# High and low part of the streamed operand in one product, for gates and scores of a two-layer mixer

## The chip, the core and the metric

The kernel runs on one core of a Trainium2 chip. The metric is the device time of one execution in microseconds, the median of several runs. One execution is also recorded by the hardware profiler; all rows shown are of that one.

## The reference, cut to what matters

Two layers over 256 tokens and 2048 channels. Each layer normalises, projects, runs an mLSTM (8 heads, keys of 128, values of 256) beside a gated linear recurrence, and projects back. The change concerns two places of the mLSTM: the input and forget gates of all heads, and the scores.

```python
p = u @ w_in
qk, v, o, z_a, ig, fg, xb, z_b = jnp.split(p, SPLIT_AT, axis=-1)
...
i_pre = ig.astype(f32) + i_bias.astype(f32)
log_f = jax.nn.log_sigmoid(fg.astype(f32) + f_bias.astype(f32))
...
sc = jnp.einsum("bhtk,bhsk->bhts", qc, kc) * jnp.exp(dmat - m_t[..., None])
num = jnp.einsum("bhts,bhsv->bhtv", sc, vc) + ...
```

`ig` and `fg` are 8 columns each of the projection. The kernel does not go chunk by chunk: it takes all 256 tokens at once, with the decay of each pair of tokens in a matrix E.

## The kernel before, in words

**Products in three parts.** Every float32 operand of TensorE is split into a high part H (rounded to the TensorE format) and a low part L, the rest. A product is H·H + H·L + L·H, summed in PSUM. ScalarE casts the high part (`wH`, line 308), VectorE subtracts for the low part (`wL`, L168, the line of the helper `tt_`).

**The stream of weights.** The weights come as units of 1 MB through SyncE's DMA queue into `raw`. A unit has two half-units, and a half-unit of a projection is 12 products of 512 columns (L332). `prepare` makes the casts and splits up to three half-units ahead of TensorE, into four buffers each for `wH` and `wL`; in the opening the first eight half-units take two casts and two splits each. A cast waits until TensorE has finished with the buffer of four half-units earlier. TensorE takes the half-units in a fixed order (`_sequence`): for each layer four groups of two heads, each with o, qk, v, xb, z, zb and the block gates (L753, 24 products of 256 a half-unit) and the output projection.

**Work beside the stream.** What follows a projection is written as generators in a queue `bg`; `pump` advances them after each half-unit, `yield` gives a cost against a budget, and `"wait"` lets the next one run. The framework then orders each engine's instructions by its own priorities, so a generator's operations stand between casts and splits in an order that the code does not fix alone.

**Gates of the heads.** `gates` lays the 16 gate columns of the weights out as 104 columns `gwp`: H of i at 0, H of f at 32, L of i at 64, L of f at 96. `gates_mm` multiplies them with the activations (`st["x"]`, 16 tiles of high and low part) into `ps_g`. `gates_gen` sums rows 0 and 64 (i) and 32 and 96 (f) after scaling by `rb`, the token's norm; then a logarithm of the sigmoid (tiles `scs`), a running sum, a running maximum, and its negative nG. nG goes out to DRAM through GpSimd's queue (`nG_d`, L538) and returns broadcast to all partitions (`nb`, L566). `e_gen` makes E from `nb` and the columns `at`: VectorE (L176), the exponential on ScalarE (L578), and the causal mask on GpSimd (L581).

**Scores.** In `qk_post`, for each of a group's two heads, six products give `ps_S`: keys are the stationary operand, queries stream, 128 keys against their 128 and 256 later tokens. VectorE multiplies by the scale and E into `Pt` (L171 is the line of the helper `stt`). `Pt` is split into PH (ScalarE, L651) and PL (VectorE), which the products `ps_n` with the values read. `ps_g`, `ps_S`, `ps_n` and the block gates' `ps_gt` take turns in four PSUM banks (`aux`).

Other names in the rows: `qc` and `xc` are the short convolutions, `vL` the low part of the values, `blk` and `tok` the transposes to channels.

Of the kernel before, what the change touches and what calls it, by code (L numbers as in the profile page):

```python
# [12 lines left out]
ALU = mybir.AluOpType  # L13
# [5 lines left out]
T = 256  # L19
KT = D // P  # L20
# [4 lines left out]
DK_SCALE = 128.0 ** -0.5  # L25
# [59 lines left out]
def tile_trunk(ctx, tc, x, xt, par, gw, gb, ws, final_g, out):  # L85
    nc = tc.nc
    V, S, G, PE = nc.vector, nc.scalar, nc.gpsimd, nc.tensor
# [9 lines left out]
    st = {"nload": 0, "credit": 0.0, "nprep": 0, "pair": 0, "aux": 0}  # L97

    def aux(name):
        st["aux"] = 1 - st["aux"]  # L100
        return psum.tile([P, 512], F32, tag=f"aux{st['aux']}", name=name, bufs=2)
# [55 lines left out]
    gbs = const.tile([NH, DEPTH, 2], F32, name="gbs")  # L157
# [9 lines left out]
    def tt_(o, a, b, op):  # L167
        return V.tensor_tensor(out=o, in0=a, in1=b, op=op)  # L168

    def stt(o, a, s, b, op0, op1):  # L170
        return V.scalar_tensor_tensor(out=o, in0=a, scalar=s, in1=b, op0=op0, op1=op1)  # L171

    def ts_(o, a, s1, op0, s2=None, op1=None):
        if s2 is None:
            return V.tensor_scalar(out=o, in0=a, scalar1=s1, scalar2=None, op0=op0)
        return V.tensor_scalar(out=o, in0=a, scalar1=s1, scalar2=s2, op0=op0, op1=op1)  # L176
# [37 lines left out]
    def order(ins, prev):  # L214
        tc.add_manual_dep(ins.ins, prev.ins.name,
                          mybir.DependencyInfo(mybir.DependencyClass.NoSync, mybir.DependencyReason.DATA),
                          reason="an order of the program")
# [276 lines left out]

    def gates_mm(l):
        ps = aux("ps_g")
        o = ps[0:104, 0:T]
        for kt in range(KT):
            gw_ = st["gwp"][kt // 8][:, kt % 8, :]
            m = PE.matmul(o, gw_, st["x"][:, kt, 0, :], start=kt == 0, stop=False)  # L500
            if kt == 0:
                order(m, st["mm"])
            PE.matmul(o, gw_, st["x"][:, kt, 1, :], start=False, stop=kt == KT - 1)  # L503
        st["ps_g"] = ps

    def gates_gen(l):
        ps, rb = st["ps_g"], st["rb", l]

        scs = work.tile([P, 8, T], F32, tag="xcs", name="scs")

        def sc(nm):
            return scs[0:NH, "ifzsd".index(nm), :]

        gi, x_ = sc("i"), sc("f")
        t_ = sc("z")
        tt_(x_, ps[32:40, 0:T], rb[32:40, :], ALU.mult)
        tt_(t_, ps[96:104, 0:T], rb[96:104, :], ALU.mult)
        stt(x_, x_, gbs[:, l, 1:2], t_, ALU.add, ALU.add)
        t_ = sc("s")
        tt_(gi, ps[0:8, 0:T], rb[0:8, :], ALU.mult)  # L520
        tt_(t_, ps[64:72, 0:T], rb[64:72, :], ALU.mult)
        tt_(gi, gi, t_, ALU.add)
        yield 0.6
        q = log1p_exp_half(x_, sc)
        yield 4
        ts_(q, q, -2.0, ALU.mult)
        stt(x_, x_, 0.0, q, ALU.min, ALU.add)
        Fc = sc("z")
        V.tensor_tensor_scan(out=Fc, data0=ones.bitcast(F32)[0:NH, 0:1].to_broadcast([NH, T]), data1=x_, initial=0.0, op0=ALU.mult, op1=ALU.add)
        sT = scs[0:64, 5, :]  # L530
        G.memset(sT, 0.0)
        stt(sT[0:8, :], gi, gbs[:, l, 0:1], Fc, ALU.add, ALU.subtract)
        Gm = sc("s")
        V.tensor_tensor_scan(out=Gm, data0=sT[0:8, :], data1=sT[0:8, :], initial=0.0, op0=ALU.max, op1=ALU.max)
        stt(sT[32:40, :], Fc, -1.0, Gm, ALU.mult, ALU.subtract)
        nG = sc("d")
        ts_(nG, Gm, -1.0, ALU.mult)
        nc.gpsimd.dma_start(out=nG_d[l], in_=nG)  # L538
        sb = scs[0:64, 6, :]
        V.transpose(out=sb, in_=sT)  # L540
        st["sb"] = sb
        st["nG", l] = True
        yield 3
# [42 lines left out]
    def mm3(o, aH, aL, bH, bL, first=True, last=True):  # L586
        PE.matmul(o, aH, bH, start=first, stop=False)  # L587
        PE.matmul(o, aH, bL, start=False, stop=False)  # L588
        PE.matmul(o, aL, bH, start=False, stop=last)  # L589
# [25 lines left out]
    def qk_post(l, g, acc):  # L615
        bg.append(e_gen(l, g))
        fr = to_channels(l, acc)

        def gen():
            for _ in range(LANDING):  # L620
                yield "wait"
            ch = joined(fr)
            yield 0.3
            qc = work.tile([P, 4, T], F32, tag="c4", name="qc", bufs=2)
            sg = work.tile([P, 4, T], F32, tag="sC", name="qsg")
            for ct in range(4):
                conv(ch, qc, ct, O_QKW + 4 * (8 * (ct % 2) + 2 * g + ct // 2), l, None)
                yield 1.2
            S.activation(out=sg, in_=qc, func=AF.Sigmoid)
            tt_(qc, qc, sg, ALU.mult)  # L630
            yield 1.2
            q = work.tile([P, 4, 2, T], F32R, tag="qs", name="qks")
            S.copy(out=q[:, :, 0, :], in_=qc)
            tt_(q[:, :, 1, :], qc, q.bitcast(F32)[:, :, 0, :], ALU.subtract)
            yield 1.2
            for _ in range(3):
                yield "wait"
            while ("E", l, g) not in st or ("v", l, g) not in st:
                yield "wait"
            E, em, so, (vH, vL) = st["E", l, g], st["em", l], st["so", l, g], st["v", l, g]  # L640
            Pt = work.tile([P, 2, 384], F32, tag="Pt", name="Pt")
            for h in range(2):
                ps = aux("ps_S")
                for o_, ss_, ts__ in ((256, slice(128, 256), slice(128, 256)), (0, slice(0, 128), slice(0, 256))):
                    mm3(ps[:, o_ : o_ + ts__.stop - ts__.start], q[:, 2 * h + 1, 0, ss_], q[:, 2 * h + 1, 1, ss_],
                        q[:, 2 * h, 0, ts__], q[:, 2 * h, 1, ts__])
                stt(Pt[:, h, :], ps[:, 0:384], DK_SCALE, E[:, h, :], ALU.mult, ALU.mult)
                yield 0.5
            PH = work.tile([P, 2, 384], F32R, tag="sD", name="PH")
            PL = work.tile([P, 2, 384], F32R, tag="sC", name="PL")  # L650
            S.copy(out=PH, in_=Pt)  # L651
            tt_(PL, Pt, PH.bitcast(F32), ALU.subtract)
            yield 1.0
            for _ in range(3):
                yield "wait"
            hh = work.tile([P, 2, 2, 256], F32, tag="sE", name="hh")
            mv = small.tile([P, 2, 2, 2], F32, tag="mv", name="mv", bufs=1)
            for h in range(2):
                pns = [aux("ps_n") for _ in range(2)]
                for t in range(2):  # L660
                    o = pns[t][:, 0:258]
                    a = slice(P * t, P * t + P)
                    mm3(o, PH[:, h, a], PL[:, h, a], vH[:, 0, h, :], vL[:, 0, h, :], last=t == 0)
                    if t == 1:
                        mm3(o, PH[:, h, 256:384], PL[:, h, 256:384], vH[:, 1, h, :], vL[:, 1, h, :], first=False)
                for t in range(2):
                    pn = pns[t]
                    dn = small.tile([P, 1], F32, tag="dn", name="dn")
                    stt(dn, pn[:, 256:257], -1.0, em[:, t, 2 * g + h : 2 * g + h + 1], ALU.mult, ALU.max)
                    tt_(dn, dn, pn[:, 256:257], ALU.max)  # L670
                    V.reciprocal(out=dn, in_=dn)
                    stt(hh[:, t, h, :], pn[:, 0:256], dn, so[:, t, 256 * h : 256 * h + 256], ALU.mult, ALU.mult)
                    bs = small.tile([P, 6], F32, tag="bs", name="bs")
                    V.bn_stats(out=bs, in_=hh[:, t, h, :])
                    V.bn_aggr(out=mv[:, t, h, :], in_=bs)
                    yield 1.1
            sd = small.tile([P, 2, 2], F32, tag="sd", name="sd", bufs=1)
            order(S.activation(out=sd, in_=mv[:, :, :, 1], func=AF.Sqrt, bias=epst), st["wH"])
            V.reciprocal(out=sd, in_=sd)
            for hd in range(2):  # L680
                for t in range(2):
                    ts_(hh[:, t, hd, :], hh[:, t, hd, :], mv[:, t, hd, 0:1], ALU.subtract, sd[:, t, hd : hd + 1],
                        ALU.mult)
            st["hn", l, g] = hh
            yield 1.0
        bg.append(gen())

    def z_post(l, g, acc):
# [396 lines left out]
    for item in dict.fromkeys(i for i, _ in seq):  # L1085
        kind, l, g = item[0], item[1], item[-1]
# [125 lines left out]
```

## Time and profile before

| | us |
|---|---|
| median of 3 runs | 1493.76 (1493.61 to 1494.64) |
| span of the profiled execution | 1491.3 |
| TensorE busy | 1481.6 |
| VectorE busy | 1050.9 |
| ScalarE busy | 925.8 |

The profiled execution's own time outside its span is not given apart; its span, from the first to the last instruction, is 2.5 us under the median of the runs. TensorE's granted clock is 0.998 of full speed over the span. Rows of the chain of work give start, duration and what ran. Rows of a timeline give start, duration, engine, line, operation, output <- input, and in brackets the idle time of the engine before it with what ended it. Rows by group give shape, count, busy time, mean duration in ns, and idle time before. A product's duration in a timeline includes its run through the array, which overlaps the next product; what a product takes on the path is seen in the chain.

### The profile page before, as it was taken

To read this page: it belongs to the slowest core of one execution; us is meant where nothing else is said; L and a number is where in the kernel's file an instruction comes from. 1 tells how busy PE (TensorE), PEld (TensorE's weight loads), DVE (VectorE), ACT (ScalarE), POOL (GpSimd) and SP (SyncE) were. 2 spreads that over 40 slices of the span, in tenths; PEclk is the share of its full clock that TensorE was granted. 3 is DMA by queue.
4 is the path that set the end of the run, shared out by engine and by line. 5 is a ranking of instruction groups with operands and counts; after the bars stand their busy time and mean duration, and the time that the engine had idled before them with its cause. 6 is when DMAs were issued, how large, how long until landed. Compare 5 with 4: busy or idle time off the path is not lost.

```text
span 1491.3 us, 18541 instructions
## 1 busy us (share of the span) xinstructions
PE 1481.6 (99%) x6894; PEld 1241.1 (83%) x6894; DVE 1050.9 (70%) x1406; ACT 925.8 (62%) x1167; POOL 81.8 (5%) x154
## 2 busy tenths in 40 slices
PE   9999999999999999999999999999999999999997
PEld 8888888888888888888888888888888888888886
DVE  6778976675567855778867798765855678556785
ACT  7656864575565855658575667645755567555675
POOL 0010100000000000000000101000000000000002
PEclk9999999999999999999999999999999999999999
DMA  9866766866677666876886666568666777577783
GB/s 337 296 224 221 227 221 208 254 224 216 199 239 232 217 225 217 258 258 226 270 277 195 231 219 240 205 205 253 223 223 216 238 223 234 200 229 265 231 282 111
DMA packets 91370, 345.66 MB, mean 232 GB/s; under 512 B 9984, under 2 KB 30480, under 8 KB 69776
## 3 DMA queue, kind: packets, MB, share of 16 engines
q1 hardware_dynamic: 79472, 306.44, 60.2%
q0 software_dynamic: 9344, 33.58, 9.1%
q10 hardware_dynamic: 2464, 4.47, 0.8%
q8 instruction: 54, 0.88, 0.2%
q14 instruction: 36, 0.29, 0.0%
HBM read 307.20 MB, written 37.24 MB: 231 GB/s over the span
## 4 chain that ended last, share of the span: by engine, by line
PE 99%; ACT 0%; DVE 0%; issue 0%; ACTq 0%
PE acc L332 89%; PE ps_gt L753 3%; PE acc L345 1%; PE acc L995 1%; PE acc L994 1%; PE acc L996 1%; PE acc_x L995 0%; PE acc_x L994 0%; PE acc_x L996 0%; PE ps_blank L110 0%; PE ps_n L589 0%; PE ps_n L587 0%; PE ps_n L588 0%; PE ps_g L500 0%; PE ps_g L503 0%; PE ps_S L588 0%
## 5 line engine op out<-in xcount | busy, mean ns | idle before, releaser
L332 PE MATMUL acc<-wH,x_s 128*128 128x512 f32 x3008 | 930.0, 389 | 0.0
L168 DVE TENSOR_TENSOR wL<-raw,wH 128x1024 fp32r<-128x1024 f32 (+1 forms) x532 | 636.5, 1204 | 341.8 <-ACT wH L308 341.3
L308 ACT CAST wH<-raw 128x1024 fp32r<-128x1024 f32 (+1 forms) x532 | 548.0, 1037 | 398.5 <-PE acc L332 367.6
L332 PEld LDWEIGHTS acc<-wH,x_s 128*128 128x128 f32 x3008 | 564.6, 188 | 116.9
L332 PE MATMUL acc<-wL,x_s 128*128 128x512 f32 x1504 | 583.9, 389 | 0.0
L332 PEld LDWEIGHTS acc<-wL,x_s 128*128 128x128 f32 x1504 | 282.3, 188 | 58.1
L332 PE MATMUL acc<-wH,yaH 128*128 128x512 f32 x224 | 87.4, 390 | 0.0
L332 PE MATMUL acc<-wH,ybL 128*128 128x512 f32 x224 | 87.3, 390 | 0.0
L332 PE MATMUL acc<-wH,yaL 128*128 128x512 f32 x224 | 87.2, 389 | 0.0
L332 PE MATMUL acc<-wL,ybH 128*128 128x512 f32 x224 | 87.2, 389 | 0.0
L332 PE MATMUL acc<-wH,ybH 128*128 128x512 f32 x224 | 87.2, 389 | 0.0
L332 PE MATMUL acc<-wL,yaH 128*128 128x512 f32 x224 | 87.2, 389 | 0.0
L332 PEld LDWEIGHTS acc<-wH,ybL 128*128 128x128 f32 x224 | 42.0, 188 | 9.1 <-DVE ybL L168 0.3
L332 PEld LDWEIGHTS acc<-wH,yaL 128*128 128x128 f32 x224 | 42.1, 188 | 9.0
L332 PEld LDWEIGHTS acc<-wH,ybH 128*128 128x128 f32 x224 | 42.1, 188 | 8.5
L332 PEld LDWEIGHTS acc<-wL,ybH 128*128 128x128 f32 x224 | 42.0, 188 | 8.5
L332 PEld LDWEIGHTS acc<-wL,yaH 128*128 128x128 f32 x224 | 42.1, 188 | 8.4
L332 PEld LDWEIGHTS acc<-wH,yaH 128*128 128x128 f32 x224 | 42.0, 188 | 8.2
L446 DVE STREAM_TRANSPOSE blk<-tok 128x1024 f32<-128x1024 f32 x33 | 40.8, 1237 | 11.0 <-ACT tok L436 11.0
L436 ACT ACTIVATE tok<-acc,rstd 128x512 f32<-128x512 f32 x46 | 29.1, 684 | 30.6 <-PE acc L332 30.6
L450 POOL DMA_DIRECT2D fr<-moved x34 | 18.9, 556 | 506.5 <-DMA moved<-blk 260.1
L892 ACT COPY stage<-acc 128x1024 f32<-128x1024 f32 x24 | 24.4, 1017 | 35.5 <-PE acc L332 35.3
(209 smaller groups left out, 1308.5 us busy)
## 6 DMA issues: line engine op xcount, KB each, us to landing
raw<-in_ws_dram SPq DMA_DIRECT2D x168, 1024.0 KB, 5.1
raw<-in_ws_dram SPq DMA_DIRECT2D x190, 512.0 KB, 4.9
fr<-moved POOLq DMA_DIRECT2D x34, 512.0 KB, 6.0
moved<-blk SPq DMA_DIRECT2D x132, 128.0 KB, 2.6
x_d<-stage POOLq DMA_DIRECT2D x24, 512.0 KB, 5.4
x_d<-x_acc ACTq DMA_DIRECT2D x8, 512.0 KB, 8.4
x_acc<-x_d SPq DMA_DIRECT2D x8, 512.0 KB, 4.4
xp<-in_xt_dram SPq DMA_DIRECT2D x8, 256.0 KB, 7.2
```

What stands on the lines that cost most here:

```text
L168: return V.tensor_tensor(out=o, in0=a, in1=b, op=op)
L308: st["wH"] = S.copy(out=H[:, o], in_=r[:, o])
L332: st["mm"] = PE.matmul(o, a_[:, kt, P * t : P * t + P], W[:, k], start=b, stop=z)
L345: PE.matmul(ps[:, ct, T * part : 2 * T], W[:, k, P * ct : P * ct + P], moving, start=first and k == 0 and part == 0, stop=last and k == 3 ...
L436: S.activation(out=by_block(tok, t), in_=acc[:, t, :].rearrange("p (c m j) -> p c m j", c=4, m=4), func=AF.Copy, scale=rstd[:, t : t + 1])
L446: V.transpose(out=blk.rearrange("p m n -> p (m n)"), in_=tok.rearrange("p m c t j -> p (m c t j)"))
L450: back.dma_start(out=fr.rearrange("p a c t i -> p a (c t i)"), in_=moved)
L753: PE.matmul(o, W[:, ib, jl], xs[:, ib, a, :], start=j == 0 and i == 0 and W is Hv and a == 0, stop=i == 1 and W is Lv, skip_group_check=True)
L892: S.copy(out=stage, in_=ps)
L994: PE.matmul(o, yH[:, kt, tsl], Hv[:, k, cs], start=start and k == 0, stop=False)
L995: PE.matmul(o, yH[:, kt, tsl], Lv[:, k, cs], start=False, stop=False)
L996: PE.matmul(o, yL[:, kt, tsl], Hv[:, k, cs], start=False, stop=stop and k == 1)
```

## The change

The high and the low part of the streamed operand lie next to each other, so one product with the same stationary operand streams both. Their results land in two halves of a PSUM bank, and the halves are added afterwards.

```diff
     def gates_mm(l):
...
-            m = PE.matmul(o, gw_, st["x"][:, kt, 0, :], start=kt == 0, stop=False)
+            m = PE.matmul(ps[0:104].rearrange("p (a t) -> p a t", a=2), gw_, st["x"][:, kt], start=kt == 0, stop=kt == KT - 1)
...
-            PE.matmul(o, gw_, st["x"][:, kt, 1, :], start=False, stop=kt == KT - 1)
...
     def gates_gen(l):
...
+        def summed(o, t_, r):
+            tt_(o, ps[r : r + 8, 0:T], rb[r : r + 8, :], ALU.mult)
+            for q0, c0 in ((r, T), (64 + r, 0)):
+                tt_(t_, ps[q0 : q0 + 8, c0 : c0 + T], rb[q0 : q0 + 8, :], ALU.mult)
+                yield t_
+
         gi, x_ = sc("i"), sc("f")
-        t_ = sc("z")
-        tt_(x_, ps[32:40, 0:T], rb[32:40, :], ALU.mult)
-        tt_(t_, ps[96:104, 0:T], rb[96:104, :], ALU.mult)
-        stt(x_, x_, gbs[:, l, 1:2], t_, ALU.add, ALU.add)
-        t_ = sc("s")
-        tt_(gi, ps[0:8, 0:T], rb[0:8, :], ALU.mult)
-        tt_(t_, ps[64:72, 0:T], rb[64:72, :], ALU.mult)
-        tt_(gi, gi, t_, ALU.add)
+        for t_ in summed(x_, sc("z"), 32):
+            tt_(x_, x_, t_, ALU.add)
+        ts_(x_, x_, gbs[:, l, 1:2], ALU.add)
+        for t_ in summed(gi, sc("s"), 0):
+            tt_(gi, gi, t_, ALU.add)
...
             for h in range(2):
-                ps = aux("ps_S")
-                for o_, ss_, ts__ in ((256, slice(128, 256), slice(128, 256)), (0, slice(0, 128), slice(0, 256))):
-                    mm3(ps[:, o_ : o_ + ts__.stop - ts__.start], q[:, 2 * h + 1, 0, ss_], q[:, 2 * h + 1, 1, ss_],
-                        q[:, 2 * h, 0, ts__], q[:, 2 * h, 1, ts__])
-                stt(Pt[:, h, :], ps[:, 0:384], DK_SCALE, E[:, h, :], ALU.mult, ALU.mult)
+                pa, pb = aux("ps_S"), aux("ps_S")
+                kH, kL = q[:, 2 * h + 1, 0], q[:, 2 * h + 1, 1]
+                for ps, ss_, ts_1 in ((pa, slice(0, 128), slice(0, 256)), (pb, slice(128, 256), slice(128, 256))):
+                    n_ = ts_1.stop - ts_1.start
+                    PE.matmul(ps[:, 0 : 2 * n_].rearrange("p (a t) -> p a t", a=2), kH[:, ss_], q[:, 2 * h, :, ts_1],
+                              start=True, stop=False, skip_group_check=True)
+                    PE.matmul(ps[:, 0:n_], kL[:, ss_], q[:, 2 * h, 0, ts_1], start=False, stop=True,
+                              skip_group_check=True)
+                for ps, o_, n_ in ((pa, 0, 256), (pb, 256, 128)):
+                    S.copy(out=Pt[:, h, o_ : o_ + n_], in_=ps[:, n_ : 2 * n_])
+                    tt_(Pt[:, h, o_ : o_ + n_], ps[:, 0:n_], Pt[:, h, o_ : o_ + n_], ALU.add)
+                stt(Pt[:, h, :], Pt[:, h, :], DK_SCALE, E[:, h, :], ALU.mult, ALU.mult)
```

In `gates_mm` the low part of the weights is now multiplied with the low part of the activations too; that quarter of `ps_g` is not read. On TensorE nothing else moves: between two pieces of changed work stand as many other products as before. On VectorE and ScalarE the order changes near the changed work. Three places:

TensorE, one head's scores, then the next product of the weight stream. Before:

```order
L587 MATMUL ps_S<-qks 128x128
L588 MATMUL ps_S<-qks 128x128
L589 MATMUL ps_S<-qks 128x128
L587 MATMUL ps_S<-qks 128x256
L588 MATMUL ps_S<-qks 128x256
L589 MATMUL ps_S<-qks 128x256
```

After (the second head's four products follow in the same way, then the weight stream):

```order
L648 MATMUL ps_S<-qks 128x512
L650 MATMUL ps_S<-qks 128x256
L648 MATMUL ps_S<-qks 128x256
L650 MATMUL ps_S<-qks 128x128
L332 MATMUL acc<-wH,x_s 128x512
```

Six products are four.

VectorE in layer 0, the end of the gates' work: L175 on `scs` gives nG, L529 or L530 and L534 or L535 are the running sum and maximum, L540 or L541 the transpose, `E` the start of the decay matrix. Before:

```order
L171 SCALAR_TENSOR_TENSOR qc<-ch,pars,qc 128x255
L171 SCALAR_TENSOR_TENSOR scs<-scs 8x256
L175 TENSOR_SCALAR scs<-scs 8x256
L540 STREAM_TRANSPOSE scs<-scs 64x256
L168 TENSOR_TENSOR wL<-raw,wH 128x1024
L171 SCALAR_TENSOR_TENSOR vL<-acc,rstd,vH 128x2x256
L171 SCALAR_TENSOR_TENSOR qc<-ch,pars,qc 128x254
L168 TENSOR_TENSOR wL<-raw,wH 128x1024
L171 SCALAR_TENSOR_TENSOR vL<-acc,rstd,vH 128x2x256
L171 SCALAR_TENSOR_TENSOR qc<-ch,pars,qc 128x253
L168 TENSOR_TENSOR wL<-raw,wH 128x1024
L176 TENSOR_SCALAR E<-nb,at_750 128x256
```

After:

```order
L171 SCALAR_TENSOR_TENSOR qc<-ch,pars,qc 128x255
L171 SCALAR_TENSOR_TENSOR scs<-scs 8x256
L171 SCALAR_TENSOR_TENSOR vL<-acc,rstd,vH 128x2x256
L530 SCALAR_TENSOR_TENSOR scs<-ones,scs 8x256
L168 TENSOR_TENSOR wL<-raw,wH 128x1024
L171 SCALAR_TENSOR_TENSOR scs<-scs,gbs 8x256
L171 SCALAR_TENSOR_TENSOR vL<-acc,rstd,vH 128x2x256
L535 SCALAR_TENSOR_TENSOR scs<-scs 8x256
L168 TENSOR_TENSOR wL<-raw,wH 128x1024
L171 SCALAR_TENSOR_TENSOR scs<-scs 8x256
L175 TENSOR_SCALAR scs<-scs 8x256
L541 STREAM_TRANSPOSE scs<-scs 64x256
```

The three splits and both `vL` that stood behind nG now stand ahead of it, and three of the short convolution's steps with them; `E` follows behind two further splits.

ScalarE in layer 0, from the second half of the convolution's starts (L418) to the exponential of E and the sigmoid behind it. Before:

```order
L551 ACTIVATE scs<-scs 32x256
L610 ACTIVATE vH<-acc,rstd 128x2x256
L308 CAST wH<-raw 128x1024
L610 ACTIVATE vH<-acc,rstd 128x2x256
L308 CAST wH<-raw 128x1024 x2
L578 ACTIVATE E<-E 128x768
L308 CAST wH<-raw 128x1024 x2
L629 ACT_TABLE_LOAD
L629 ACTIVATE qsg<-qc 128x1024
```

After:

```order
L611 ACTIVATE vH<-acc,rstd 128x2x256
L308 CAST wH<-raw 128x1024
L611 ACTIVATE vH<-acc,rstd 128x2x256
L308 CAST wH<-raw 128x1024 x2
L552 ACTIVATE scs<-scs 32x256
L308 CAST wH<-raw 128x1024 x2
L579 ACTIVATE E<-E 128x768
L308 CAST wH<-raw 128x1024
L630 ACT_TABLE_LOAD
L630 ACTIVATE qsg<-qc 128x1024
```

Two casts of the weight stream that stood behind the exponential of E now stand ahead of it.

More of the change, by code (lines that the diff above doesn't have):

```diff
@@ L496, in gates_mm @@
         ps = aux("ps_g")
-        o = ps[0:104, 0:T]
         for kt in range(KT):
             gw_ = st["gwp"][kt // 8][:, kt % 8, :]
-            m = PE.matmul(o, gw_, st["x"][:, kt, 0, :], start=kt == 0, stop=False)
+            m = PE.matmul(ps[0:104].rearrange("p (a t) -> p a t", a=2), gw_, st["x"][:, kt], start=kt == 0, stop=kt == KT - 1)
             if kt == 0:
                 order(m, st["mm"])
-            PE.matmul(o, gw_, st["x"][:, kt, 1, :], start=False, stop=kt == KT - 1)
         st["ps_g"] = ps
```

## The prediction

> **What bounds the kernel now.** I read the page first, then the chain of work that ended last in order of time, then the groups by shape, and last the timelines of VectorE, ScalarE and GpSimd around the first gates. The page:
>
> ```profile
> span 1491.3 us, 18541 instructions
> PE 1481.6 (99%) x6894; PEld 1241.1 (83%) x6894; DVE 1050.9 (70%) x1406; ACT 925.8 (62%) x1167; POOL 81.8 (5%) x154
> PE 99%; ACT 0%; DVE 0%; issue 0%; ACTq 0%
> L168 DVE TENSOR_TENSOR wL<-raw,wH 128x1024 fp32r<-128x1024 f32 (+1 forms) x532 | 636.5, 1204 | 341.8 <-ACT wH L308 341.3
> L308 ACT CAST wH<-raw 128x1024 fp32r<-128x1024 f32 (+1 forms) x532 | 548.0, 1037 | 398.5 <-PE acc L332 367.6
> ```
>
> The chain is 99% TensorE. ScalarE's casts (wH) idle because TensorE has not yet given a weight buffer back, and VectorE (wL) waits for the casts: both normally run ahead. So this change can gain only products that TensorE no longer issues, and can lose only where a split comes late. What a product costs on the path is read from the chain, start, duration and count:
>
> ```profile
> 7.28 21.81 PE acc L332 x96
> 32.88 16.35 PE acc L332 x72
> 49.46 62.58 PE acc L332 x276
> 113.42 10.93 PE acc L332 x48
> 145.56 5.60 PE ps_gt L753 x48
> 312.71 130.59 PE acc L332 x576
> 701.66 89.97 PE acc L332 x396
> 795.43 2.75 PE acc L332 x12
> ```
>
> A 512-column product takes 130.59/576 = 226.7 ns, a 256-column one 5.60/48 = 116.7 ns. The holes are the work that changes: gates of layer 0 from 29.09 to 32.88, 3.79 us (118 ns for each of 32); gates of layer 1 from 791.63 to 795.43, 3.80; one group's scores from 112.04 to 113.42, 1.38 for 12 products, so 115 ns each, though half of them have only 128 columns.
>
> **Gates on TensorE.** In each layer 32 products of 256 become 16 of 512: 16 x 0.2267 = 3.63 against 3.79 and 3.80. Saved: 0.16 + 0.17 = 0.33 us.
>
> **Scores on TensorE.** The columns are unchanged (1152 per head); six products become four: 512, 256, 256 (two strips of 128) and 128. With 115 ns for the last, a head takes 0.2267 + 2 x 0.1167 + 0.115 = 0.575, a group 1.15. Saved: 0.23 per group, 1.84 us in eight. No row shows a 128-column product among wider ones only. Bounds: it may hide down to its columns, about 0.06 us (half of 116.7 ns), which adds 16 x 0.055 = 0.9 of gain; or the 115 ns was not a price per product and the gain is zero. I take 115, the row of this very block. The two-strip form has no row either; I give it the 256-column price.
>
> The Trainium skill ("TensorE: Matmul & The Clock Gate", section "Back-to-back issue gap") gives N/2.4 + 2.5 ns for an isolated product: 55.8, 109.2 and 215.8 for 128, 256 and 512 columns. By that the score block is 0.99 before and 0.98 after, and nothing is gained; this is a rival below. The trace disagrees: the block takes 1.38. The same page's section "LDWEIGHTS (loading the stationary operand)" has a load grow with its 128 columns alone, 107 ns, which is near the 115 measured.
>
> **What is added elsewhere.** Groups by shape, with count, busy time and mean:
>
> ```profile
> L758 ACT ACTIVATE gate<-ps_gt,pars 128x256 f32<-128x256 f32 x64 | 26.3, 490 | 2.0 <-PE ps_gt L753 2.0
> L578 ACT ACTIVATE E<-E 128x768 f32<-128x768 f32 x8 | 6.8, 848 | 6.6 <-DVE E L176 6.5
> L168 DVE TENSOR_TENSOR x_acc<-x_acc,acc 128x256 f32<-128x256 f32 x2 | 0.8, 422 | 1.8 <-PE acc L996 1.8
> L171 DVE SCALAR_TENSOR_TENSOR Pt<-ps_S,E 128x384 f32<-128x384 f32 x16 | 8.7, 544 | 5.9 <-PE ps_S L589 5.9
> L168 DVE TENSOR_TENSOR wL<-raw,wH 128x1024 fp32r<-128x1024 f32 x516 | 625.4, 1220 | 338.8 <-ACT wH L308 338.5
> L171 DVE SCALAR_TENSOR_TENSOR vL<-acc,rstd,vH 128x512 fp32r<-128x512 f32 x16 | 12.0, 747 | 6.9 <-ACT vH L610 6.8
> L171 DVE SCALAR_TENSOR_TENSOR qc<-ch,pars,qc 128x255 f32<-128x255 f32 x32 | 14.5, 476 | 1.9 <-ACT qc L418 1.9
> L168 DVE TENSOR_TENSOR scs<-ps_g,rb 8x256 f32<-8x256 f32 x8 | 3.3, 418 | 0.2
> L168 DVE TENSOR_TENSOR scs<-scs 8x256 f32<-8x256 f32 x6 | 2.4, 403 | 0.0
> L175 DVE TENSOR_SCALAR scs<-scs 8x256 f32<-8x256 f32 x8 | 2.2, 280 | 1.2 <-ACT scs L184 1.1
> L171 DVE SCALAR_TENSOR_TENSOR scs<-scs,gbs 8x256 f32<-8x256 f32 x4 | 1.9, 466 | 0.0
> ```
>
> *Scores.* Each group adds four ScalarE copies out of PSUM, at most 4 x 0.49 = 2.0 us (L758's form; the 128-wide ones will be less), and four VectorE additions, at most 4 x 0.42 = 1.7; the two multiplications by E stay at 0.54. Behind them queue the casts and splits, and ps_n, which needs PH and PL. Both have cover in the first group, one of the fullest:
>
> ```profile
> 117.92 0.96 DVE L168 TENSOR_TENSOR PL<-Pt,PH 128x768 fp32r<-128x768 f32 x1
> ```
>
> PL ends at 118.88; ps_n starts behind 48 products, at 113.42 + 10.93 = 124.35. The 5.5 us of cover takes the 1.7 of additions and one split (1.22) that now stands ahead of PL, with 2.5 over. The tiles cannot hold TensorE: four aux buffers exist, a group now takes four, and ps_n's four come 10.9 us later. Path cost: zero. If the cover failed, 8 groups would each pay the excess.
>
> *Gates.* VectorE had per layer 4 x 0.418 + 0.466 + 0.403 = 2.54 us from ps_g to both sums; now 6 x 0.418 + 4 x 0.403 + 0.280 = 4.40, so +1.86. TensorE does not read these sums. But they lead, through nG, two DMAs on GpSimd's queue (nG_d out, nb back) and E, to a place where ScalarE and VectorE stand still with casts and splits behind them. Layer 0, VectorE and then GpSimd:
>
> ```profile
> 53.74 1.22 DVE L168 TENSOR_TENSOR wL<-raw,wH 128x1024 fp32r<-128x1024 f32 x1
> 64.91 1.21 DVE L168 TENSOR_TENSOR wL<-raw,wH 128x1024 fp32r<-128x1024 f32 x1
> 66.05 0.40 DVE L168 TENSOR_TENSOR scs<-scs 8x256 f32<-8x256 f32 x1
> 76.74 0.28 DVE L175 TENSOR_SCALAR scs<-scs 8x256 f32<-8x256 f32 x1
> 86.84 1.01 DVE L176 TENSOR_SCALAR E<-nb,at 128x256 f32<-128x256 f32 x4 [3.80 <-DMA nb<-nG_d]
> 93.83 1.22 DVE L168 TENSOR_TENSOR wL<-raw,wH 128x1024 fp32r<-128x1024 f32 x1
> ...
> 77.33 0.53 POOL L538 DMA_DIRECT2D nG_d<-scs  x1 [12.93 <-DVE scs L175]
> 80.97 0.55 POOL L566 DMA_DIRECT2D nb<-nG_d  x1 [3.11 <-DMA nG_d<-scs]
> ```
>
> nG ends at 77.02 and E starts at 86.84, after 9.82 us of DMA. By the new order more work stands ahead of nG than the five extra operations: three more splits (3.66), both vL (1.49) and three more qc (1.43). Sum 1.86 + 3.66 + 1.49 + 1.43 = 8.4 for 13 operations. Consecutive rows overlap by 0.07 (64.91 + 1.21 against 66.05), which takes 0.9 off: nG ends 7.5 later, at 84.5, and E starts at 94.3.
>
> Against that, ScalarE and VectorE now do two more casts and splits ahead of E. The first split behind it is the one that began at 93.83. It is number 39 from 0; the first eight half-units took two splits each, so it serves half-unit 31, due after 31 x 12 = 372 products. 168 were done by 49.46; the other 204 at 62.58/276 put it at 95.7, or 95.5 with the faster gates. Now E (1.01) and the split (1.22) end at 94.3 + 2.23, less two overlaps, 96.4. TensorE waits 0.9. The next split: exponential 0.85, cast 1.04, split 1.22 behind E's 95.3 end at 98.4; due 2.72 after the last, 98.2 plus the 0.9: no more wait. With layer 1's DMA time below, 7.1, E would start at 91.6 and nothing would wait. I take the row of the same place, 0.9.
>
> ```profile
> 826.54 0.28 DVE L175 TENSOR_SCALAR scs<-scs 8x256 f32<-8x256 f32 x1
> 833.96 1.01 DVE L176 TENSOR_SCALAR E<-nb,at 128x256 f32<-128x256 f32 x4 [2.17 <-DMA nb<-nG_d]
> 836.83 2.40 DVE L168 TENSOR_TENSOR wL<-raw,wH 128x1024 fp32r<-128x1024 f32 x2 [0.72 <-ACT wH L308]
> ```
>
> In layer 1 only one qc (0.47) more stands ahead of nG, so it comes about 2 us later, and one split that stood behind E now stands ahead of it: 2.7 us of respite. Cost zero.
>
> **Sum.** -0.33 - 1.84 + 0.9 = -1.3 us. The profiled execution's span is 1491.3; the median of the three timed runs, 1493.76, is 2.5 above it, and I let that lie around the span unchanged: 1490.0 of span, 1492.5 of time. What this measurement can tell from no change is about 0.2%, 3 us.
>
> **Rivals.**
> 1. *No wait in layer 0*: the DMAs take 7 to 9 us. E before 93.4 hides all. For it: layer 1's 7.1; against: 9.8 at the place itself. -2.2: 1491.6.
> 2. *Products cost columns*: the score block's 115 ns is not a price per product, so scores save nothing (by the page's gap formula, named above). Against it: 1.38 for 12. -0.33 + 0.9: 1494.3.
> 3. *Slower, E far too late*: nG, the DMAs or the cast chain slip further. From E at 98.6 on, TensorE waits 5.2 and the net loss passes 3 us. That needs 4.3 us more than I found, for instance nb landing that much later on a queue that weights keep busy. At 5 more: wait 5.9, +3.7: 1497.5.
> 4. *Faster*: the 128-column product hides (-0.9 more) and nothing waits: -3.1, 1490.7.
> 5. *Scores' cover fails*: PL over 2.5 us later than I count in every group; at 3.5, 8 x 1.0 more: 1500.5. Against it: the rows above.
>
> **Numbers.** My forecast 0.45 (its own range 1491.7 to 1494), rival 1 0.27, rival 2 0.08, rival 3 0.08, rival 4 0.07, rival 5 0.05. The range reaches from rival 4 to past rival 2, into part of rival 3, with 0.3 for the measurement below: 1490.4 to 1495.8. Faster by over 0.2%: most of rival 4, 0.06. Slower: rivals 3 and 5, 0.12. Same: 0.82.
>
> **What would show it.** The holes in the chain: gates 3.63, scores 1.15 per group. VectorE's nG in layer 0 near 84.5 and E near 94, with ScalarE and VectorE idle ahead of it; TensorE waiting for a wL at about 95.5, under 2 us, and nowhere else; rows from the gates of layer 0's first group on equal but for a shift. Wrong is the prediction if TensorE waits behind the scores, or if the score block stays near 1.38.

## The result, and the profile after

The changed kernel takes 1491.15 us, the median of 19 runs (1490.44 to 1491.97), the kernel before 1493.85 (1493.08 to 1495.18, 19 runs): a ratio of 0.998, 95% interval 0.9973 to 0.9987. In a second comparison it was 1491.13 against 1493.39: 0.9985, 0.9976 to 0.9994. The change gains 2.3 to 2.7 us, just within the 0.2% that the prediction counted as no change. The time lies in its range, 1.35 us under its value. The profiled execution of a repeat of the kernel before, used further down, had a granted clock of 0.85 and a span of 1643.7 us, so that no trace of that repeat can be read.

The page of the profiled execution: span, busy times, and the engines' shares of the chain.

```profile
span 1489.5 us, 18487 instructions
PE 1479.5 (99%) x6830; PEld 1236.0 (83%) x6830; DVE 1060.1 (71%) x1448; ACT 931.6 (63%) x1199; POOL 83.1 (6%) x154
PE 96%; DVE 2%; DMA 1%; ACT 1%; issue 0%; POOL 0%; SPq 0%; DVEq 0%; ACTq 0%; POOLq 0%
```

TensorE has 64 products fewer. VectorE is 9.2 us busier and ScalarE 5.8, and the span is shorter all the same. The new shares of VectorE (2%), DMA (1%) and ScalarE (1%) say that the chain left TensorE once. The chain in order of time:

```profile
6.80 21.81 PE acc L332 x96
28.61 3.71 PE ps_g L499 x16
32.32 16.36 PE acc L332 x72
...
112.59 10.97 PE acc L332 x48
...
202.71 13.71 PE acc L332 x59
...
790.92 3.71 PE ps_g L499 x16
```

The gates take 3.71 us in each layer (before 3.79 and 3.80), and a score block, from 111.49 to 112.59, takes 1.10 (before 1.38). The row at 202.71 is the one place where the chain comes back from another engine. The list of TensorE's waits (us in all, how often, the longest) names it, the chain leads to a transfer, and ScalarE's timeline shows the copy that waits for that:

```profile
PE acc L332 <- DVE wL L168: 0.4, 1, 0.4
183.34 9.05 DMA fr<-moved
192.41 1.05 ACT L470 COPY ch<-fr 128x1024 f32<-128x1024 f32 x1 [5.57 <-DMA fr<-moved]
```

ScalarE stands at `ch` (L470) until `fr`, the transposed queries and keys of the second group, has come, and the casts behind it come late. The 288 products between the block gates' end (150.39) and the scores (216.42) took 66.03 us. So 0.73 is lost, of which the list of waits has 0.4, since it counts from the modelled end of the product before. The prediction has no such wait. Before, the copy waited 3.99 us for the transfer and the products took 65.30:

```profile
191.63 1.05 ACT L470 COPY ch<-fr 128x1024 f32<-128x1024 f32 x1 [3.99 <-DMA fr<-moved]
151.16 65.30 PE acc L332 x288
```

Where it did forecast a wait, at 95 us, there is none. VectorE's rows of the gates' chain in layer 0, then GpSimd's:

```profile
83.36 0.28 DVE L175 TENSOR_SCALAR scs<-scs 8x256 f32<-8x256 f32 x1
91.28 1.01 DVE L176 TENSOR_SCALAR E<-nb,at 128x256 f32<-128x256 f32 x4 [2.16 <-DMA nb<-nG_d]
83.95 0.53 POOL L539 DMA_DIRECT2D nG_d<-scs  x1 [21.64 <-DVE scs L175]
85.88 0.55 POOL L567 DMA_DIRECT2D nb<-nG_d  x1 [1.40 <-DMA nG_d<-scs]
```

nG ends at 83.64, and E starts 7.64 us later, where before it took 9.82. TensorE's list has no wait but the one at 203 us and one for the first operand of all.

### The profile page after: what moved, and what is told of

It is laid out like the page before. It is cut to its first block, busy times and chain, and to the rows that moved or that the text cites. A ratio compares the mean times of both kernels' runs of the same rounds, so it can differ in the third digit from the quotient of the medians.

```text
span 1489.5 us, 18487 instructions
## 1 busy us (share of the span) xinstructions
PE 1479.5 (99%) x6830; PEld 1236.0 (83%) x6830; DVE 1060.1 (71%) x1448; ACT 931.6 (63%) x1199; POOL 83.1 (6%) x154
## 4 chain that ended last, share of the span: by engine, by line
PE 96%; DVE 2%; DMA 1%; ACT 1%; issue 0%; POOL 0%; SPq 0%; DVEq 0%; ACTq 0%; POOLq 0%
PE acc L332 86%; PE ps_gt L761 3%; PE acc L345 2%; DVE wL L168 1%; DMA fr<-moved 1%; PE acc L1004 1%; PE acc L1003 1%; PE acc L1002 1%; PE ps_g L499 0%; PE acc_x L1004 0%; PE acc_x L1003 0%; PE acc_x L1002 0%; PE ps_S L648 0%; PE ps_n L590 0%; PE ps_n L588 0%
## 5 line engine op out<-in xcount | busy, mean ns | idle before, releaser
L171 DVE SCALAR_TENSOR_TENSOR xc<-ch,pars,xc 128x255 f32<-128x255 f32 (+2 forms) x96 | 43.0, 475 | 4.4 <-ACT xc L420 4.4
```

## Experiments

Theory A: what TensorE no longer issues is the gain, score and gate parts add up, and the wait at 203 us depends on when `fr` lands, not on the change. Rival B: the gain comes from the gates' part or the order that it changes. Rival C, in two places: the wait is caused by the changed order; or columns, not products, are what the scores pay.

**Both kernels again, and each half of the change alone.** The first two are unedited. The third has the diff's part in `qk_post` alone, the fourth its parts in `gates_mm` and `gates_gen` alone:

```diff
 # scores alone: gates_mm and gates_gen as before
+                pa, pb = aux("ps_S"), aux("ps_S")
...
 # gates alone: qk_post as before
+            m = PE.matmul(ps[0:104].rearrange("p (a t) -> p a t", a=2), gw_, st["x"][:, kt], start=kt == 0, stop=kt == KT - 1)
...
```

> The kernel before, unchanged, run as one of five so that the others have a second profile of it beside them. A: its time equals that of the kernel before within the measurement. The profile tells how much two executions of one program differ: in the first product's start (7.28 us before), in nG's way through DRAM in layer 0 (9.82 us), and in the landing of the fr transfer of the second group's queries and keys (about 7.5 us). If the start moves by 0.5 us between two profiles of one program, then the 0.48 us by which the changed kernel's first product started earlier is no effect of the change.

> The changed kernel again, unchanged. A (products that TensorE does not issue are the gain, waits are the noise): score blocks 1.10 us, gates 3.71 us in each layer as in the first profile; TensorE's wait for a split at about 203 us, 0.6 us long in the first profile, comes or not as the fr transfer lands late or not, so it may be gone here; time 2.0 to 2.7 us under the kernel before. C (the wait is caused by the changed order of ScalarE and VectorE): the wait stands at the same place with 0.4 to 0.8 us in this profile too.

> Only the scores are changed (four products a head, the copies and additions), the gates are as before. A: score blocks 1.10 us against 1.38, and the 48 products behind each about 0.04 us longer, so 0.24 us for each of eight groups: 1.9 us under the kernel before, that is about 0.2 us behind the changed kernel. The gates take 3.79 us a layer. B (the gain comes from the gates or from the order that they change): not over 0.5 us under the kernel before.

> Only the gates are changed (16 products of 512 columns a layer, and the longer sum on VectorE), the scores are as before. A: gates 3.71 us against 3.79 in each layer, 0.17 us in all, which the timing can hardly tell from nothing: 0 to 0.5 us under the kernel before. nG comes some 7 us later than before in layer 0, as in the changed kernel, and E's first operation ends in time all the same, if the way through DRAM takes 7 to 8 us; if it takes 9.8 as in the first profile of the kernel before, TensorE waits 0.9 us near 95 us. B (the gates' order is what moved the time): 1.5 us or more under the kernel before.

| | median us, runs | ratio to before, 95% |
|---|---|---|
| before, again | 1493.43, 12 (1493.16, 11, without the execution named above) | 1.0001 (0.9992 to 1.001) |
| changed, again | 1491.13, 11 | 0.9985 (0.9976 to 0.9994) |
| scores alone | 1491.53, 11 | 0.9988 (0.998 to 0.9997) |
| gates alone | 1493.20, 11 | 0.9999 (0.9991 to 1.0008) |

Against 1493.39 the scores alone gain 1.86 us, the gates alone 0.19, both together 2.26. The parts add up within what the timing can tell, and B falls. The gates alone are the one kernel whose runs lie 2.03 to 2.15 us above their spans, the others 1.66 to 1.78. By the medians of the spans (1491.7 before, 1491.1 for the gates alone) they gain 0.6, which the timing cannot tell from 0.19. Why this kernel differs is not known.

The chains around 145 to 218 us: the changed kernel again, then the scores alone, then the gates alone. The 288 products run from the end of `ps_gt` to the first `ps_S`.

```profile
29.20 3.71 PE ps_g L499 x16
145.36 5.60 PE ps_gt L761 x48
150.96 65.30 PE acc L332 x288
216.26 0.23 PE ps_S L648
```

```profile
10.13 19.38 PE acc L332 x84
145.74 5.62 PE ps_gt L760 x48
184.32 9.21 DMA fr<-moved
217.56 0.23 PE ps_S L647
```

```profile
29.04 3.71 PE ps_g L499 x16
145.44 5.62 PE ps_gt L754 x48
184.01 8.95 DMA fr<-moved
216.96 0.06 PE ps_S L588
```

The same changed kernel does without the wait when `fr` lands sooner. The scores alone lose 217.56 - 151.36 - 65.30 = 0.90 us, the gates alone 0.60. Set by landing time, from GpSimd's issue to ScalarE's copy:

| kernel | landing us | lost us | gates start | span | rest |
|---|---|---|---|---|---|
| before | 7.50 | 0 | 29.09 | 1491.3 | 1462.2 |
| changed | 9.07 | 0.73 | 28.61 | 1489.5 | 1460.2 |
| changed, again | 6.74 | 0 | 29.20 | 1489.4 | 1460.2 |
| scores alone | 9.24 | 0.90 | 29.51 | 1490.7 | 1460.3 |
| gates alone | 8.97 | 0.60 | 29.04 | 1491.7 | 1462.1 |

"Rest" is the span less the opening (up to the gates' start) and the loss. It differs by kernel alone: 1462.2 less 0.17 for the gates is 1462.0, less 1.92 for the scores 1460.3, less both 1460.1, each within 0.1 of its row. The opening moves by 0.9 us between the profiles and by 0.59 between the two of the changed kernel, so the 0.48 of its first profile need not be an effect of the change. The wait goes by the landing: each half of the change has it without the other, and the whole change has it in one execution and not in the next. That the change makes late landings more frequent is not ruled out, since the two profiles with the order of before (the first, 7.50, and the next experiment's, 8.40) show no wait.

**Narrow products made wide.** In the kernel before, the three products of 128 columns of each head stream 256; the rest of the work is as it was, and the added columns are not read.

```diff
-                for o_, ss_, ts__ in ((256, slice(128, 256), slice(128, 256)), (0, slice(0, 128), slice(0, 256))):
...
+                qf = q.rearrange("p a b t -> p (a b t)")
+                for o_, ss_, t0 in ((256, slice(128, 256), 128), (0, slice(0, 128), 0)):
+                    at = 1024 * h + t0
...
+                        qf[:, at : at + 256], qf[:, at + 256 : at + 512])
```

> The kernel before with one thing changed: in each head the three score products of 128 columns stream 256 columns (the 128 more lead into PSUM columns that nothing reads). Products stay twelve a group. A (a product of 128 columns costs what one of 256 does, about 115 ns): score blocks stay at 1.38 to 1.41 us, time equal to the kernel before within 0.3 us. C (columns are what is paid): 6 products of a group get 128 columns more, 0.055 us each, so blocks near 1.7 us and 2.6 us more in eight groups.

Measured 1493.57 us, ratio 0.9999 (0.999 to 1.0008). The chain of one block: the first four products in the kernel before and in this kernel, and the second to the fifth in the changed kernel (its second profile). Columns are start, duration and what ran:

```profile
216.47 0.06 PE ps_S L587
216.52 0.11 PE ps_S L588
216.64 0.11 PE ps_S L589
216.75 0.17 PE ps_S L587
```

```profile
217.01 0.12 PE ps_S L587
217.12 0.12 PE ps_S L588
217.24 0.12 PE ps_S L589
217.36 0.12 PE ps_S L587
```

```profile
216.49 0.12 PE ps_S L650
216.61 0.12 PE ps_S L648
216.73 0.06 PE ps_S L650
216.78 0.28 PE ps_S L648
```

A narrow product alone takes 0.06 us, but the product behind it takes 0.05 more than it would (0.17 for 256 columns, 0.28 for 512). With 256 columns all are 0.12, and the block is 1.43 (217.01 to 218.44), where 1.38 stood and columns would give 1.7. So products are paid, and the 128 more columns of each are nearly free.

**E made late.** The changed kernel with twelve small copies on GpSimd ahead of the transfer `nb` of layer 0's first group:

```diff
...
+        if (l, g) == (0, 0):
+            for _ in range(12):
+                last = G.tensor_copy(out=idle, in_=st["nGt"][:, 0:16])
...
```

> The changed kernel with twelve small copies (8x16, into a tile that nothing reads) on GpSimd ahead of the transfer that brings nG back in layer 0's first group; the order on ScalarE, VectorE and TensorE stays. By GpSimd's copies of the trace (4.15 us for eight) they take 6.2 us and put the transfer some 4.8 us later, so E starts near 96 instead of 91.3. A (E is in line with the casts and splits, whose cover there was 1.8 us): TensorE waits 3.0 us for a split near 95 us, time 3.0 us over the changed kernel, that is 0.7 us over the kernel before. D (E's lateness is absorbed by the splits that run ahead): no wait there, time as the changed kernel.

Measured 1495.22 us, 1.0011 (1.0002 to 1.002): 4.1 over the changed kernel. GpSimd's transfer, VectorE's E, and TensorE's waits:

```profile
92.59 0.55 POOL L572 DMA_DIRECT2D nb<-nG_d  x1
96.20 1.01 DVE L176 TENSOR_SCALAR E<-nb,at 128x256 f32<-128x256 f32 x4 [6.21 <-DMA nb<-nG_d]
PE acc L332 <- DVE wL L168: 2.5, 2, 2.2
PE ps_n L597 <- DVE PL L168: 0.8, 1, 0.8
```

E starts 4.35 us later than in the changed kernel's second profile (96.20 against 91.60, less 0.25 for the later opening). TensorE waits 2.2 for a split at about 96 to 98 us, where the prediction put its wait. The prediction's own sum, with E at 96.20, has that split end at 98.3 (96.20 + 1.01 + 1.22 less two overlaps of 0.07), and TensorE goes on at 98.40. A is right about the place, and 3.0 was expected. But the lateness does not end there: the first block gates start 3.53 us late (149.14 - 29.45 = 119.69 us behind the gates, against 116.16), with 0.8 of it in the wait for PL, the stretch behind them loses another 0.64, and the total is above A's 3.0. D, by which the splits that run ahead absorb the lateness, falls.

**The transfer on another queue.** The changed kernel with the second group's `fr` issued by SyncE, so that it no longer stands behind GpSimd's masks of E (by the table above the waits so far cost 0.60 to 0.90 us, not up to 1.1):

```diff
-        fr = to_channels(l, acc)
+        fr = to_channels(l, acc, nc.sync if g == 1 else G)
```

> The changed kernel with one transfer moved to another queue: fr of the second group's queries and keys goes through SyncE's queue instead of GpSimd's, where it stood behind E's four masks. In three of five profiles so far TensorE waited 0.6 to 1.1 us near 203 us behind this transfer, where it took 9 us or more from issue to the copy that reads it; where it took 7.5 us or less nothing waited. A: it starts about 2 us earlier, the copy comes before 192 us in layer 0, the wait is gone, and the median is 0.3 to 0.8 us under the changed kernel with less scatter. C (the wait comes from something else, or the transfer now stands behind a weight unit on SyncE's queue): the wait stays or grows, median equal or above.

Measured 1491.12 us (1490.58 to 1491.37, 11 runs), 0.9984 (0.9975 to 0.9993). SyncE's issue, ScalarE's copy, and the stretch:

```profile
182.25 0.34 SPq L450 DMA_DIRECT2D fr<-moved  x1
190.35 1.05 ACT L470 COPY ch<-fr 128x1024 f32<-128x1024 f32 x1
151.25 65.31 PE acc L332 x288
```

The copy stands before 192, ScalarE no longer idles ahead of it, and the stretch is 65.31. The scatter is smaller, 0.79 us between the extremes where the changed kernel's second comparison had 1.50 (1490.43 to 1491.93), of 11 runs each. But the median is that of the changed kernel, 1491.13: the expected 0.3 to 0.8 did not come. This execution waited 0.7 us for a cast of the opening instead. No version here beats the changed kernel by what can be measured.

**How much cover the scores' added work has.** The changed kernel with each copy of score halves five times over:

```diff
-                    S.copy(out=Pt[:, h, o_ : o_ + n_], in_=ps[:, n_ : 2 * n_])
+                    for _ in range(5):
+                        S.copy(out=Pt[:, h, o_ : o_ + n_], in_=ps[:, n_ : 2 * n_])
```

> The changed kernel with each copy of score halves on ScalarE done five times over instead of once: sixteen more copies a group, 8 x 0.38 + 8 x 0.29 = 5.4 us of ScalarE per group between the scores and PH. It asks how much cover the added work of the scores has. A (PL is the limit: it ended 3.0 us before TensorE needed it in the first group and 4.5 us in the others): TensorE waits 2.4 us for ps_n in the first group and about 0.9 us in each of the others, 9 us in all over the changed kernel, and no wait where the cover holds. E (casts and splits queued behind the copies come late too): waits on weight splits as well, over 15 us in all. D (the order adapts, or the cover is larger): under 3 us.

Measured 1491.30 us, 0.9985 (0.9976 to 0.9994): D, the order adapts or the cover is larger. ScalarE's copies of the first group and VectorE's PL, in the changed kernel (second profile) and then in this one:

```profile
113.08 0.97 ACT L653 COPY Pt<-ps_S 128x256 f32<-128x256 f32 x4
120.25 0.95 DVE L168 TENSOR_TENSOR PL<-Pt,PH 128x768 fp32r<-128x768 f32 x1
```

```profile
113.31 4.54 ACT L654 COPY Pt<-ps_S 128x256 f32<-128x256 f32 x20
120.78 0.95 DVE L168 TENSOR_TENSOR PL<-Pt,PH 128x768 fp32r<-128x768 f32 x1
```

The copies take 3.57 us more, 0.23 each rather than the 0.29 and 0.38 of the means, and PL comes only 0.3 later, measured from the gates' start. In the changed kernel ScalarE idled after the copies and then did three convolutions (`xc`) ahead of PH; here these come after PH. So the order adapted, and the experiment did not find the end of the cover.

## Why the prediction was right, and where it was wrong

- *TensorE bounds the kernel, and only products no longer issued can gain*: right. The two halves add up in the times, and with opening and wait set aside the five profiles leave no other term above 0.1 us. The two terms, 0.17 and 1.92, make 2.09 us; the comparisons gave 2.70 and 2.26, with intervals from 1.9 to 4.0 and from 0.9 to 3.6 us, so the 0.2 to 0.6 that is left is within the noise.
- *Gates, -0.33*: half as much, -0.17. The step that failed is the price: 226.7 ns came from the weight stream, and the 16 products here take 3.71/16 = 231.9 ns. Why they cost more was not tried.
- *Scores, -1.84*: -1.92. A block saves 0.28 and the 48 products behind it take 10.97 instead of 10.93, so 0.24 in each of eight groups. That 115 ns was a price per product was right. The upper bound was wrong in its picture: the narrow product does hide down to 0.06, but the next pays it back. So rivals 2 and 4 (the latter's 0.9 for the hidden product) fall. Of the Trainium skill's page "TensorE: Matmul & The Clock Gate", the section "Back-to-back issue gap" would have given no saving by its isolated gap, of which it says itself that it counts too little for narrow products in a stream of loads and products. The trace disagrees by 1.9 us. The rule of that page's section "LDWEIGHTS (loading the stationary operand)" gives 107 ns for 128 columns, an estimate. That is near the 0.115 to 0.12 of every block, though no run separates a load from its product, so why a narrow product has this price stays open.
- *Gates' longer sum, nG 7.5 us later*: right. nG ended at 83.64 with an opening 0.48 shorter, 84.1 in the frame of before, for 84.5.
- *E 9.82 us behind nG, so a wait of 0.9*: the step that failed. The hop is no property of the place but of the moment. Asked for at the old time it took 9.82, 9.69 and 9.67 us in the three profiles with the old gates (before, scores alone, products made wide); asked for 7 us later it took 7.21 to 7.64 in the five with the new gates whose transfer was not held back. The traffic differs. Two stretches, the first of before, the second of after: behind the times stand the busy time of PE, PEld, DVE, ACT and POOL, then the granted clock, the DMA engines' share, and GB/s.

```profile
78.00:80.00 2.00, 2.00 (x11) 1.65 (x10) 1.91 (x4) 2.00 (x4) 0.00 (x0) 1.00 0.88 346
```

```profile
84.00:86.00 2.00, 2.00 (x11) 1.65 (x10) 2.00 (x4) 1.47 (x2) 0.60 (x2) 1.00 0.28 111
```

  In the first, nG_d goes out beside a weight unit, and GpSimd waits 3.11 us for 8 KB; in the second it waits 1.40. So rival 1 came true, for which I had given 0.27, and its 1491.6 is near the 1491.15. The range held the time, but the forecast's own value counted a wait that did not come. The transfer that the twelve copies held back points the same way as the two rows: `nb` took 3.6 us from issue to E at a DMA share of 0.31 (92.59 to 96.20), and 5.4 at 0.75 in the changed kernel (85.88 to 91.28). VectorE stood still in the former, so this pair alone does not tell traffic from VectorE's work; in the two rows VectorE was busy in both (1.91 and 2.00 us of 2.00). That traffic is the cause is argued from these rows; no run changed the traffic alone. The Trainium skill ("DMA: Bandwidth & Descriptors", section "Latency and other measured facts") has memory answer in 0.2 us on average and 2 us at high load; the 1.7 us between the two rows goes the same way.
- *Rival 3's mechanism* is real, as the twelve copies show: E 4.35 us late costs 2.2 at the place, and 4.1 in the end. The prediction's price for the place itself holds; in total it was too low, since it let nothing pass on, neither to the first group's PL nor to the second group.
- *Scores' cover, cost zero*: right. PL ended at 120.61, and `ps_n` began at 123.56, 2.95 later, for 2.5 forecast.
- *Waits nowhere else; rows from layer 0's first group on equal but for a shift*: wrong, through the transfer `fr`. The profile of before had it land in 7.50 us, and I took that one row for the rule; between 5.97 and 9.24 occur, and TensorE waits from 8.97 on and not up to 8.40. Four of the eight usable profiles in which GpSimd issues it have this wait.
- *The time around the span, 2.5 us*: mis-sized by 0.8. Each run here has its span beside its time, and the difference is 1.66 to 1.77 us in all 30 of the changed kernel and 1.66 to 1.72 in the repeat of before. By that the profiled execution of before took about 1493.0 us, an estimate, since its own time is not on record, and was a quick one: none of the 19 runs of the first comparison is below 1493.08, and the medians of the later ones are 1493.39 and 1493.27. What a median run has beyond it no trace shows. Together with the absent wait, 0.9, this is a little more than the 1.35 by which the forecast was high; the gates, dearer by 0.16, went the other way.

## What to carry to other kernels

On a TensorE-bound chain like this one, where every product loads its own stationary operand (6894 products and 6894 loads), count products, not columns, below 256 columns: read the price of a narrow product together with the one behind it. A small DRAM hop took 9.7 or 7.4 us here by the moment of its request: where a change moves the request, take a range of hops and not the row of the same place. When a gain is 0.2%, split off the opening and the waits that vary between executions before comparing two spans.

## What had not been expected of the hardware

- A product of 128 columns took 0.06 us and the next 0.05 more than its own price, whether that has 256 or 512 columns.
- One transfer of 512 KB at the same place of the same program took 6.74 us in one execution and 9.07 in another.
- GpSimd's eight copies into `at` took 4.15 us mostly beside a busy VectorE, and 1.85 with E made late, where VectorE stood still. Of the twelve copies, the first is in the chain with 4.19 us, while VectorE worked (until 89.99), and the last ten with 0.20 each. They were to put E's transfer 4.8 us later and put it 6.1 later (92.59 against 86.48). E still came only 4.60 later (4.35 without the later opening): from the transfer's issue to E it was 3.6 us, where it had been 5.1.
